# A hybrid decoder layer on one Trainium2 core: the triangular substitution of the gated DeltaNet goes from VectorE to GpSimd, with the v transposes behind the scores and four smaller edits

## The chip, the cores and the metric

One core of one Trainium2 chip runs the whole layer in one launch. The metric is the time of one execution on the device in microseconds; 0.2% of it (5 us) is about the least change that can be told from none.

The core's engines have their own in-order queues: TensorE (PE: matmuls and transposes), VectorE (DVE), ScalarE (ACT), GpSimd (POOL) and SyncE (SP, which here issues the DMAs). An instruction starts when it is at the head of its queue and what it needs is there.

## The reference, cut to what matters

2048 prompt tokens and 64 sample tokens (8 sequences of 8) go through one layer of width 1024, all in fp32:

```python
mod = silu(c) @ w_ada + b_ada                      # sh1, sc1, g1, sh2, sc2, g2
h = rmsnorm(x) * (1 + sc1) + sh1
qkv, z, b_raw, a_raw, sq, sk, sv = split(h @ w_in)
# (A) gated DeltaNet, 4 heads of 128, per chunk of C tokens:
A = where(strict, beta * (k @ k.T) * decay, 0)
T = inverse(I + A)                                 # unit lower triangular
u = T @ (v * beta) - (T @ (k * beta * exp(G))) @ S
o = (q * exp(G)) @ S + ((q @ k.T) * decay) @ u
S = S * c_dec + k_tail.T @ u
# (B) sliding-window attention, 8 q heads, 2 kv heads, window 128, sinks, relative bias
x = x + g1 * (concat(rmsnorm(o) * silu(z), attention) @ w_out)
h = rmsnorm(x) * (1 + sc2) + sh2
gate, up = split(conv3(h @ w_up) + b)              # 2 x 2816 columns
x = x + g2 * ((silu(gate) * up) @ w_down)
y = rmsnorm(x)
```

The convolutions' and the DeltaNet's states and the attention's caches are outputs as well. The part that this change moves belongs to `T = inverse(I + A)`.

## The kernel before

The tokens are worked on in two halves, in blocks of (512, 512) and of (384, 384, 320) columns. A matrix product in fp32 is done as three: each operand is split into a rounded part (`w_hi`, `hi`, by ScalarE) and the rest (`w_lo`, `lo`, by VectorE or GpSimd, line 362 for the weights), and hi·hi, lo·hi and hi·lo are summed in PSUM (line 370). In the profile `in_ps` is the in-projection, `op_ps` the out-projection, `up_ps` the up-projection of the ConvFFN. Its last columns go by a scheme of quarters (`uq_...`), for which GpSimd early and VectorE later form sums of the down-projection's weights (`weight_sums`: a unit loads `suv`, does four additions and stores `ws_d`; 11 units over `KH`).

The stages, in us of the profiled execution: start, adaLN vectors and first blocks of the in-projection 0 to 110; in-projection of half 1, with `weight_sums` on GpSimd, to 240; the first chunk's `front` and `levels` ("ahead") to 300; the mixers of half 1 beside the in-projection of half 2, to 745; out-projection of half 1 to 890; ahead and mixers of half 2 beside up-projections, then the sample tokens, to 1390; up to 1530; out-projection of half 2 to 1640; more up, then the quarters to 2110; down-projection to the end.

In the mixers, chunk c of 128 tokens runs `scan(c)` (the DeltaNet's recurrence), `attend(c)`, `levels(c+1)` and `front(c+2)` in lockstep: they are generators, one step of each in turn, and `beside` draws projection steps (the "filler") between them by a share. What is written so is input to a scheduler with a timeline of its own that then fixes the order in each engine's queue by the durations it assumes. An instruction can so land ahead of or behind others than the code says.

`front(c)` is where the change is. In order: loads `kq` (k and q, line 691) and `xv` (693); `gm` on GpSimd (697); transposes of k and q (705) and their norms (`ss`, `nr` by a power on GpSimd, 714); decays `d_ps` (724) and `Dc` (728); transposes of v (`v_ps`) and `vb`; the scores `am_ps` (744), scaled by VectorE to `AM`; `AM` to DRAM (`at_d`, 755) and back (`G`, 760) so that the eight 16 × 16 diagonal blocks of each of 4 heads stand on 32 partitions. There the unit triangular blocks are inverted by substitution: `TU` is set to the identity (memsets, GpSimd, 765, 766), its first column filled (767), then for each of 14 columns a product `gt` (772) and a subtraction into `TU` (774), each of which needs the one before, and a transposed copy (777). `TU` goes to DRAM (`tu_d`, 784, 8 DMAs) and comes back in two gathers, `T` and `inv` (799, 8 DMAs). `levels` builds the whole inverse out of these blocks in three doublings: `z_ps` and `u_ps` (line 819), where the first z needs `T<-tu_d`.

The chunk's `TU`, `G` and `xv` have one buffer each, `AM` and `vb` two, `kq` three. The product's GpSimd work in the mixers is `gm`, `nr`, `Dc`, `o` (946), `dv` (999), `PT` (1040, an operand of the attention's `pv_ps`), the convolution's small copies (586, 589) and one in ten weight splits.

Of the kernel before, what the change touches and what calls it, by code (L numbers as in the profile page):

```python
# [30 lines left out]
H = 4  # L31
# [63 lines left out]
def kernel(  # L95
# [57 lines left out]
    def ada_init(pool, tmp):  # L153
        craw = tmp.tile([P, KT, 9], F32, tag="craw", name="craw")
        nc.scalar.dma_start(craw, I["cT"])
        cT = pool.tile([P, KT, 32], F32, tag="cT", name="cT")
        bT = pool.tile([P, 48], F32, tag="bT", name="bT")
        nc.vector.memset(cT, 0.0)
        nc.scalar.activation(cT[:, :, 0:9], craw, AF.Silu)
        nc.scalar.dma_start(bT, I["b_adaT"])  # L160
        return cT, bT
# [194 lines left out]
    def load_split(src, eng=None, out=None):  # L356
        return split(load_raw(src), eng, out)
# [96 lines left out]
    def gates(hf, h, wb, pool):  # L454
# [8 lines left out]
        for bi, c0, n, np_ in blocks(hf):  # L463
# [5 lines left out]
            ev = gw.tile([P, 512], F32, tag="cv", name="ba_ev", bufs=CV)  # L469
            nc.scalar.copy(ev[:32, :n], pb[:32, :n])  # L470
            yield True
# [14 lines left out]
        nc.sync.dma_start(dt, I["dn_dt_bias"][0].partition_broadcast(P))  # L486
        nc.scalar.activation(al, al, AF.Exp)
        t0, t1, t2 = [pool.tile([P, NCH // 2 + 1, H], F32, tag=t, name=t)[:, :n_] for t in ("t0", "t1", "t2")]
# [194 lines left out]
    def front(c, d, pool, rows=P):  # L683
# [48 lines left out]
        yield True  # L732
        v_ps = bank("v_ps", "fr")
        for h in range(H):
            nc.tensor.transpose(v_ps[:rows, P * h:P * h + P], xv[:, h, :], ident)
        vb = pool.tile([P, H, P], F32, tag="vb", name="vb", bufs=two)
        nc.vector.tensor_tensor(vb[:rows], heads(v_ps)[:rows], over_i(nr[:rows, :, 0], P), ALU.mult)
        yield True

        AM = pool.tile([P, H, 2, rows], F32, tag="AM", name="AM", bufs=1 if smp else 2)  # L740
# [18 lines left out]
        for h in range(H):  # L759
            nc.sync.dma_start(G[nb * h:nb * h + nb], bass.AP(a0.tensor, a0.offset + h * rows,  # L760
                                                             [[BS * ap_ + BS, nb], [ap_, BS], [1, BS]]))
        yield True
        TU = pool.tile([4 * P // BS, 2, BS, BS], F32, tag="TU", name="TU", bufs=1)
        T0 = TU[:np_, 0]
        nc.gpsimd.memset(T0, 0.0)
        nc.gpsimd.memset(T0.rearrange("p i j -> p (i j)")[:, ::BS + 1], 1.0)
        nc.vector.tensor_scalar_mul(T0[:, 1:, 0], G[:np_, 0, 1:], -1.0)
        for j in range(1, BS - 1):
            shape = [np_, BS - 1 - j, j + 1]
            tm = pool.tile([4 * P // BS, BS * BS // 4], F32, tag="gt", name="gt")  # L770
            tv = tm[:np_, :shape[1] * shape[2]].rearrange("p (i k) -> p i k", i=shape[1])
            nc.vector.tensor_tensor(tv, G[:np_, j, j + 1:].unsqueeze(2).broadcast_to(shape),
                                    T0[:, j, 0:j + 1].unsqueeze(1).broadcast_to(shape), ALU.mult)
            nc.vector.tensor_tensor(T0[:, j + 1:, 0:j + 1], T0[:, j + 1:, 0:j + 1], tv, ALU.subtract)
            if j % 5 == 0:
                yield True
        nc.vector.tensor_copy(TU[:np_, 1], T0.rearrange("p i j -> p j i"))
        t0 = (tu_s if smp else tu_d[par])[0:1]
# [453 lines left out]
    def out_weights(hf):  # L1232

        seq = [m for o in OUT_ORDER[:len(HALVES[hf])] for m in o]
        w = {m: load_split(I["w_outT"][m]) for m in seq[:2]}
        for i, m in enumerate(seq):
            yield w[m]
            if m not in seq[i + 1:i + 3]:
                del w[m]
                new = next((x for x in seq[i + 1:] if x not in w), None)  # L1240
                if new is not None:
                    w[new] = load_split(I["w_outT"][new])
            yield
# [183 lines left out]

    RING, RING_T = 6, 1

# [3 lines left out]
    def copy_consts(dst, src):  # L1433
        for t in ("cw", "cb"):
            nc.gpsimd.tensor_copy(dst[t], src[t])
        nc.gpsimd.tensor_copy(dst["out"][:, 2 * PLAIN:], src["out"][:, 2 * PLAIN:])

# [490 lines left out]
    SHARE = (5.4, 5.5, 4.0, 2.05, (2.0, 1.4), 5.0, (1.3, 2.0), 8.0)  # L1928
    PLAIN = 3

    gate = cp.tile([P, NCH + 1, H], F32, tag="gate", name="gate")
# [9 lines left out]
    with ExitStack() as main:  # L1941
# [12 lines left out]
        with ExitStack() as es:  # L1954
# [71 lines left out]
            for bi in range(2):  # L2026
                for m in range(2):
# [5 lines left out]
            chain(*[spaced(ada_cols([(c, k + q) for q in range(4)], ac, st, at_bank), 2) for c in range(2, 6) for k in (0, 4)],  # L2033
                  spaced(weight_sums(range(6), sa, nc.gpsimd), 2)),
            chain(bias_tables(sa), gates(0, h, ic["wb"], ip), *[x_rstd(1, bi, rBs[bi], sa, st_bank) for bi in range(3)]))
# [69 lines left out]
        with ExitStack() as es:  # L2105
            sp = new_pool(es, "sp", side="right")
            beside(lockstep(sample_delta(sp), sample_attend(sp), weight_sums(range(6, KH), sp, nc.vector)), filler, SHARE[2])
        with ExitStack() as es:
            up_tags[:] = FREE_TAGS
            filler, h = between(1, filler, es, range(2 * PLAIN))  # L2110
        with ExitStack() as es:
# [5 lines left out]
            with ExitStack() as es2:  # L2117
                ts = new_pool(es2, "ts", side="right")
                beside(chain(token_sums(q, ts), W.first(PLAIN)), filler, SHARE[7])
                rest(filler)  # L2120
            uc2 = {t: tq.tile(list(a.shape), F32, tag=f"u{t}", name=f"u{t}") for t, a in uc[0].items()}
            copy_consts(uc2, uc[0])
# [107 lines left out]
```

## Time and profile before

| | |
|---|---|
| median of 3 runs | 2585.77 us (2584.51 to 2588.64) |
| profiled execution | 2588.13 us, span 2586.4 us |
| granted TensorE clock | 0.994 |
| instructions in the span | 45302 |
| TensorE busy | 2515.8 us, 97% |
| VectorE busy | 1811.4 us, 70% |
| ScalarE busy | 1286.7 us, 50% |
| GpSimd busy | 763.9 us, 30% |
| DMA | 427.62 MB, 165 GB/s over the span |

A time of the table is that of a whole execution; the span is from the first to the last instruction, 1.7 us less. Busy time counts the time in which an engine has an instruction of its own under way, not whether the end waits for it. In the rows of the profile, PE is TensorE, PEld its weight loads, DVE VectorE, ACT ScalarE, POOL GpSimd, and SPq a DMA issue of SyncE; a group's row ends, behind the mean duration in ns, with the idle time ahead of it and what ended that.

### The profile page before, as it was taken

What the parts mean: (1) busy time and instruction counts of PE and PEld (TensorE: products, weight loads), DVE (VectorE), ACT (ScalarE), POOL (GpSimd) and SP (SyncE); (2) the same over time, 40 slices, a digit from 0 to 9 for tenths busy, and PEclk for the clock granted to TensorE, in tenths of its full rate; (3) what the DMA queues carried; (4) which work ended last, traced back from release to release, by engine and by line L of the source; (5) the groups of instructions that cost most, each with busy time, mean ns of one, the idle gap of its engine ahead of it and who ended that gap; (6) DMA issues with size and microseconds to landing.
All of it is one profiled execution on the core that took longest, in us unless ns stands there. A gap on an engine that the chain in (4) does not pass through costs nothing.

```text
span 2586.4 us, 45302 instructions
## 1 busy us (share of the span) xinstructions
PE 2515.8 (97%) x16410; PEld 2211.3 (85%) x16410; DVE 1811.4 (70%) x3621; ACT 1286.7 (50%) x3133; POOL 763.9 (30%) x697
## 2 busy tenths in 40 slices
PE   7999999999999999999999999999999999999998
PEld 5777888888988787787887789999999998888998
DVE  6465579897543677788758665886776666687676
ACT  5554365554343455465544353655555554454453
POOL 2064143323232422222111123345555520021012
PEclk9999999999999999999999999999999999999999
DMA  7887553343555353443346267325555448676463
GB/s 278 281 297 255 159 141 112 101 120 93 128 178 203 109 150 96 107 104 100 88 163 200 80 219 225 112 78 164 174 174 183 160 168 293 213 242 201 138 193 133
DMA packets 315852, 427.62 MB, mean 165 GB/s; under 512 B 82243, under 2 KB 206244, under 8 KB 315364
## 3 DMA queue, kind: packets, MB, share of 16 engines
q1 hardware_dynamic: 315052, 423.55, 51.8%
q8 instruction: 129, 2.11, 0.3%
q0 software_dynamic: 288, 1.11, 0.1%
q14 instruction: 95, 0.78, 0.1%
q10 hardware_dynamic: 288, 0.06, 0.0%
HBM read 305.07 MB, written 120.57 MB: 165 GB/s over the span
## 4 chain that ended last, share of the span: by engine, by line
PE 75%; DVE 11%; DMA 6%; ACT 3%; issue 2%; POOL 2%; SPq 1%; DVEq 0%; POOLq 0%; ACTq 0%
PE up_ps L370 19%; PE dn_ps L1850 17%; PE in_ps L370 8%; PE op_ps L370 6%; PE uq_b L1632 6%; PE uq_c L1632 3%; DVE ev L581 3%; PE uq_u L1632 2%; PE uq_g L1632 2%; PE uq_a L1632 1%; PE as_ps L1009 1%; DMA wada<-in_w_ada_dram 1%; PE pv_ps L1047 1%; PE u_ps L819 1%; DVE w_lo L362 1%
## 5 line engine op out<-in xcount | busy, mean ns | idle before, releaser
L370 PE MATMUL in_ps<-hi,w_hi 128*128 128x512 f32 (+2 forms) x880 | 319.4, 366 | 2.5 <-ACT hi L301 1.9
L370 PE MATMUL in_ps<-lo,w_hi 128*128 128x512 f32 (+2 forms) x880 | 315.6, 359 | 3.1 <-DVE lo L302 2.0
L370 PE MATMUL up_ps<-hi,w_hi 128*128 128x512 f32 (+2 forms) x808 | 313.0, 388 | 1.5 <-ACT sg L576 1.5
L370 PE MATMUL in_ps<-hi,w_lo 128*128 128x512 f32 (+2 forms) x880 | 314.0, 357 | 0.5 <-POOL w_lo L362 0.5
L370 PE MATMUL up_ps<-lo,w_hi 128*128 128x512 f32 (+2 forms) x808 | 312.1, 387 | 1.9 <-DVE lo L302 1.9
L370 PE MATMUL up_ps<-hi,w_lo 128*128 128x512 f32 (+2 forms) x808 | 311.0, 386 | 0.1
L1850 PE MATMUL dn_ps<-tl,wh 128*128 128x512 f32 (+2 forms) x796 | 271.6, 341 | 0.0
L1850 PE MATMUL dn_ps<-th,wh 128*128 128x512 f32 (+2 forms) x796 | 269.9, 341 | 0.0
L1850 PE MATMUL dn_ps<-th,wl 128*128 128x512 f32 (+2 forms) x796 | 268.7, 341 | 0.0
L361 ACT CAST w_hi<-w_raw 128x1024 fp32r<-128x1024 f32 x126 | 132.1, 1049 | 145.9 <-PE op_ps L370 63.0
L362 DVE TENSOR_TENSOR w_lo<-w_raw,w_hi 128x1024 fp32r<-128x1024 f32 x115 | 145.3, 1264 | 84.1 <-ACT w_hi L361 78.3
L370 PEld LDWEIGHTS in_ps<-lo,w_hi 128*128 128x128 f32 x880 | 166.9, 190 | 23.1 <-issue 3.4
L370 PEld LDWEIGHTS in_ps<-hi,w_hi 128*128 128x128 f32 x880 | 166.2, 190 | 23.2 <-issue 3.6
L370 PEld LDWEIGHTS up_ps<-hi,w_hi 128*128 128x128 f32 x808 | 152.3, 188 | 35.2 <-issue 7.3
L370 PEld LDWEIGHTS up_ps<-lo,w_hi 128*128 128x128 f32 x808 | 152.4, 189 | 33.4 <-issue 6.4
L370 PEld LDWEIGHTS in_ps<-hi,w_lo 128*128 128x128 f32 x880 | 166.5, 189 | 15.9 <-issue 1.0
L370 PEld LDWEIGHTS up_ps<-hi,w_lo 128*128 128x128 f32 x808 | 152.1, 188 | 27.9 <-issue 1.6
L1734 ACT CAST wh<-wr 128x512 fp32r<-128x512 f32 x149 | 92.2, 619 | 154.8 <-PE dn_ps L1850 101.6
L581 DVE SCALAR_TENSOR_TENSOR ev<-rb,cw,ev 128x512 f32<-128x512 f32 (+2 forms) x180 | 142.6, 797 | 35.2 <-ACT ev L574 31.5
L1850 PEld LDWEIGHTS dn_ps<-tl,wh 128*128 128x128 f32 x796 | 150.5, 189 | 15.7 <-DVE tl L1735 0.3
L1850 PEld LDWEIGHTS dn_ps<-th,wl 128*128 128x128 f32 x796 | 150.4, 189 | 15.2
L1850 PEld LDWEIGHTS dn_ps<-th,wh 128*128 128x128 f32 x796 | 150.2, 189 | 15.5
(574 smaller groups left out, 6414.6 us busy)
## 6 DMA issues: line engine op xcount, KB each, us to landing
w_raw<-in_w_upT_dram SPq DMA_DIRECT2D x50, 512.0 KB
wada<-in_w_ada_dram SPq DMA_DIRECT2D x48, 512.0 KB
w_raw<-in_w_inT_dram SPq DMA_DIRECT2D x44, 512.0 KB
wr<-ws_d SPq DMA_DIRECT2D x88, 256.0 KB
w_raw<-in_w_outT_dram SPq DMA_DIRECT2D x34, 512.0 KB
d<-act_d SPq DMA_DIRECT2D x33, 512.0 KB
wr<-in_w_downT_dram SPq DMA_DIRECT2D x66, 256.0 KB
proj<-ev SPq DMA_DIRECT2D x44, 256.0 KB
```

What stands on the lines that cost most here:

```text
L361: nc.scalar.copy(hi, raw)
L362: (eng or nc.vector).tensor_tensor(lo, raw, hi.bitcast(F32), ALU.subtract)
L370: nc.tensor.matmul(ps[:, :n], a[:, k, :], b[:, k, :n], start=first is not False and k == ks[0] and i == 0, stop=last is not False and k == ...
L581: nc.vector.scalar_tensor_tensor(out, src(j), w[:, j:j + 1], out, ALU.mult, ALU.add)
L819: mm = lambda out, a, b, r, c: nc.tensor.matmul(out, a, b, start=True, stop=True, tile_position=(r, c))
L1009: nc.tensor.matmul(banks[v][:, 256 * g:256 * g + 256 - P * k0], qs[:, 2 * (g0 + g) + v], t[:, v, :2 - k0].rearrange("p w j -> p (w j)"), s ...
L1047: mm = nc.tensor.matmul(pv_ps[64 * v:64 * v + 64, :], (vprev[0], vt if k0 else dv)[half][:, 64 * v:64 * v + 64], PT[v, half], start=half = ...
L1632: nc.tensor.matmul(bk[t][:, :nb], u[:, k], v[:, k], start=new and k == 0 and y == 0, stop=k == KG - 1 and y == 2, skip_group_check=True)
L1734: nc.scalar.copy(h, raw)
L1850: nc.tensor.matmul(acc[m, s][:, :n], w[q, i][a][:, c], th[b][:, v], start=new and i == 0 and y == 0, stop=i == KH - 1 and y == 2, skip_gro ...
```

## The change

1. `front`: the v transposes and `vb` stand behind the scores, the store of `at_d` and the loads of `G`.
2. `front`: the substitution's 1 first column, 28 products and subtractions and 1 transposed copy go from VectorE to GpSimd (17 calls: 16 chunks and the sample).
3. At the start ScalarE takes a Silu of a constant before `craw` has come in; in `gates` the Exp of `al` is held behind the copy `held`. Both change which tables ScalarE loads: in its program the loads go from 13 to 10.
4. `out_weights`: in the second half every other of the later `w_out` splits has its `w_lo` on GpSimd (8 of them).
5. `RING_T` 1 → 2: two weight tiles of the quarters are prepared ahead instead of one. `uc2["out"]` shrinks to the part that is copied.
6. `FEW = 5`: five units of weight sums on GpSimd at the start (six before), the other six on VectorE beside the sample's steps.

```diff
+        warm = tmp.tile([P, 16], F32, tag="warm", name="warm")
+        nc.scalar.activation(warm, mhalf, AF.Silu)
...
-            nc.scalar.copy(ev[:32, :n], pb[:32, :n])
+            held = nc.scalar.copy(ev[:32, :n], pb[:32, :n]).ins
...
-        nc.scalar.activation(al, al, AF.Exp)
+        with tc.issue_after(held):
+            nc.scalar.activation(al, al, AF.Exp)
...
-        v_ps = bank("v_ps", "fr")
-        for h in range(H):
-            nc.tensor.transpose(v_ps[:rows, P * h:P * h + P], xv[:, h, :], ident)
-        vb = pool.tile([P, H, P], F32, tag="vb", name="vb", bufs=two)
-        nc.vector.tensor_tensor(vb[:rows], heads(v_ps)[:rows], over_i(nr[:rows, :, 0], P), ALU.mult)
-        yield True
...
             nc.sync.dma_start(G[nb * h:nb * h + nb], bass.AP(a0.tensor, a0.offset + h * rows,
                                                              [[BS * ap_ + BS, nb], [ap_, BS], [1, BS]]))
         yield True
+        v_ps = bank("v_ps", "fr")
+        for h in range(H):
+            nc.tensor.transpose(v_ps[:rows, P * h:P * h + P], xv[:, h, :], ident)
+        vb = pool.tile([P, H, P], F32, tag="vb", name="vb", bufs=two)
+        nc.vector.tensor_tensor(vb[:rows], heads(v_ps)[:rows], over_i(nr[:rows, :, 0], P), ALU.mult)
+        yield True
...
-        nc.vector.tensor_scalar_mul(T0[:, 1:, 0], G[:np_, 0, 1:], -1.0)
+        nc.gpsimd.tensor_scalar(T0[:, 1:, 0], G[:np_, 0, 1:], -1.0, 1.0, ALU.mult, ALU.mult)
...
-            nc.vector.tensor_tensor(tv, G[:np_, j, j + 1:].unsqueeze(2).broadcast_to(shape),
+            nc.gpsimd.tensor_tensor(tv, G[:np_, j, j + 1:].unsqueeze(2).broadcast_to(shape),
                                     T0[:, j, 0:j + 1].unsqueeze(1).broadcast_to(shape), ALU.mult)
-            nc.vector.tensor_tensor(T0[:, j + 1:, 0:j + 1], T0[:, j + 1:, 0:j + 1], tv, ALU.subtract)
+            nc.gpsimd.tensor_tensor(T0[:, j + 1:, 0:j + 1], T0[:, j + 1:, 0:j + 1], tv, ALU.subtract)
...
-        nc.vector.tensor_copy(TU[:np_, 1], T0.rearrange("p i j -> p j i"))
+        nc.gpsimd.tensor_copy(TU[:np_, 1], T0.rearrange("p i j -> p j i"))
...
-                    w[new] = load_split(I["w_outT"][new])
+                    w[new] = load_split(I["w_outT"][new], nc.gpsimd if hf and i % 2 else None)
...
-    RING, RING_T = 6, 1
+    RING, RING_T = 6, 2
...
-        nc.gpsimd.tensor_copy(dst["out"][:, 2 * PLAIN:], src["out"][:, 2 * PLAIN:])
+        late = lambda a: a[:, a.shape[1] - MU + 2 * PLAIN:]
+        nc.gpsimd.tensor_copy(late(dst["out"]), late(src["out"]))
...
+    FEW = 5
...
-                  spaced(weight_sums(range(6), sa, nc.gpsimd), 2)),
+                  spaced(weight_sums(range(FEW), sa, nc.gpsimd), 2)),
...
-            beside(lockstep(sample_delta(sp), sample_attend(sp), weight_sums(range(6, KH), sp, nc.vector)), filler, SHARE[2])
+            beside(lockstep(sample_delta(sp), sample_attend(sp), weight_sums(range(FEW, KH), sp, nc.vector)), filler, SHARE[2])
```

All lines behind the first edit move by 2 to 5 numbers: the substitution's lines 765 to 777 are 767 to 779 in the changed kernel, `kq`'s load 694, `nr` 717, `Dc` 731, `PT` 1042, `dv` 1001.

How the queues change, at two places. The first is VectorE's queue in the second half's mixers, before, from the first column of chunk 14's substitution on (`ss`, `bn`, `r` belong to the norms of this and another chunk):

```order
L767 TENSOR_SCALAR TU<-G 32x15
L143 TENSOR_SCALAR rsq<-ss_13230 128x4
L772 TENSOR_TENSOR gt<-G,TU 32x28
L774 TENSOR_TENSOR TU<-TU,gt 32x14x2
L712 TENSOR_SCALAR ss<-ss 128x8
L772 TENSOR_TENSOR gt<-G,TU 32x39
L716 RECIPROCAL bn<-ss 128x4
L774 TENSOR_TENSOR TU<-TU,gt 32x13x3
L717 TENSOR_TENSOR bn<-bn,beta 128x4
L772 TENSOR_TENSOR gt<-G,TU 32x48
L945 TENSOR_TENSOR r_13239<-r_13239,nr 128x4
L718 TENSOR_TENSOR bn<-bn,tail 128x4
```

Other VectorE work stands between the steps of the chain. GpSimd's queue in the changed kernel, at the end of the same chunk's substitution:

```order
L776 TENSOR_TENSOR TU<-TU,gt 32x4x12
L1042 TENSOR_TENSOR PT<-pt,cst 128x512
L774 TENSOR_TENSOR gt<-G,TU 32x39
L717 TENSOR_TENSOR nr<-ss,halves 128x8
L776 TENSOR_TENSOR TU<-TU,gt 32x3x13
L731 TENSOR_TENSOR Dc<-Dc,cst 128x512
L774 TENSOR_TENSOR gt<-G,TU 32x28
L1042 TENSOR_TENSOR PT<-pt,cst 128x512
L776 TENSOR_TENSOR TU<-TU,gt 32x2x14
L774 TENSOR_TENSOR gt<-G,TU 32x15
L776 TENSOR_TENSOR TU<-TU,gt 32x15
L779 COPY TU<-TU 32x256
```

The chain now shares its queue with `PT`, `nr` and `Dc`, which stood there before without it.

The second place is SP's queue ahead of the load of the first chunk's k and q, before (`suv` and `ws_d` are the load and the store of a weight-sums unit, `proj<-ev` a store of the in-projection):

```order
L1676 DMA suv<-in_w_downT_dram 128x1024 x2
L353 DMA w_raw<-in_w_inT_dram 128x1024
L643 DMA proj<-ev 128x512 x2
L1685 DMA ws_d<-suv 128x1024 x2
L353 DMA w_raw<-in_w_inT_dram 128x1024
L691 DMA kq<-proj 128x4x128 x2
L693 DMA xv<-proj 128x4x128
```

and in the changed kernel:

```order
L646 DMA proj<-ev 128x512
L1688 DMA ws_d<-suv 128x1024 x2
L646 DMA proj<-ev 128x512
L355 DMA w_raw<-in_w_inT_dram 128x1024
L646 DMA proj<-ev 128x512
L694 DMA kq<-proj 128x4x128 x2
L696 DMA xv<-proj 128x4x128
```

The sixth unit's load and store are gone from here; three other DMAs now stand between the fifth unit's store and `kq`, where one stood behind the sixth's.

More of the change, by code (lines that the diff above doesn't have):

```diff
@@ L2120 @@
                 rest(filler)
-            uc2 = {t: tq.tile(list(a.shape), F32, tag=f"u{t}", name=f"u{t}") for t, a in uc[0].items()}
+            shape = lambda t, a: [P, MU - 2 * PLAIN, 18] if t == "out" else list(a.shape)
+            uc2 = {t: tq.tile(shape(t, a), F32, tag=f"u{t}", name=f"u{t}") for t, a in uc[0].items()}
             copy_consts(uc2, uc[0])
```

## The prediction

> **What bounds the kernel now.** I read the busy shares first, then the table by stage, then what TensorE (PE) waits for in each stage, and last one chunk's chain in order of time.
>
> ```profile
> PE 2515.8 (97%) x16410; PEld 2211.3 (85%) x16410; DVE 1811.4 (70%) x3621; ACT 1286.7 (50%) x3133; POOL 763.9 (30%) x697
> 300.00:745.00 445.00, 426.21 (x3545) 385.90 (x3544) 326.31 (x946) 227.48 (x736) 131.04 (x132) 0.99 0.43 120
> 890.00:1300.00 410.00, 406.86 (x3060) 327.21 (x3060) 329.80 (x905) 221.85 (x700) 91.12 (x89) 0.99 0.41 107
> ```
>
> The first row is the whole span, the other two (length, then busy PE, PEld, DVE, ACT, POOL, granted clock, DMA share, GB/s) are the mixers of the first and of the second half. TensorE is busy 97% of the span. VectorE (DVE) has 326.3 of 445.0 us in the first mixers and 329.8 of 410.0 in the second, GpSimd (POOL) 131.0 and 91.1. Taking work off VectorE can pay only where TensorE waits for VectorE; those waits, the first mixers' and then the second's (total us, times, longest):
>
> ```profile
> PE u_ps L819 <- DVE Y L869: 4.1, 2, 3.0
> PE z_ps L819 <- DVE T L842: 3.5, 2, 2.3
> PE pv_ps L1047 <- POOL PT L1040: 2.2, 2, 1.4
> PE z_ps L819 <- DVE T L861: 2.1, 3, 1.4
> PE o_ps L921 <- DVE S L915: 1.8, 2, 1.1
> PE pt_ps L1036 <- DVE nl L1029: 1.6, 2, 1.1
> PE o_ps L901 <- DVE vb L896: 1.1, 1, 1.1
> PE ot_ps L951 <- POOL o L946: 0.6, 1, 0.6
> ...
> PE z_ps L819 <- DMA T<-tu_d: 0.5, 1, 0.5
> ```
> ```profile
> PE o_ps L901 <- DVE vb L896: 0.5, 1, 0.5
> ```
>
> Six VectorE rows of the first mixers sum to 14.2 us (4.1 + 3.5 + 2.1 + 1.8 + 1.6 + 1.1); in the second mixers it is 0.5. So the most that a freer VectorE can give there is 14.7 us, 0.6% of the time, and the substitution's own chain hardly shows: `T<-tu_d`, its last transfer, costs 0.5 us in all.
>
> **The substitution, moved.** Removed from VectorE:
>
> ```profile
> L774 DVE TENSOR_TENSOR TU<-TU,gt 32x28 f32<-32x28 f32 (+5 forms) x238 | 58.5, 246 | 4.8
> L772 DVE TENSOR_TENSOR gt<-G,TU 32x28 f32<-32x28 f32 (+5 forms) x238 | 55.8, 234 | 4.9
> L767 DVE TENSOR_SCALAR TU<-G 32x15 f32<-32x15 f32 (+1 forms) x17 | 7.1, 417 | 18.1 <-DMA G<-at_d 18.0
> L777 DVE COPY TU<-TU 32x256 f32<-32x256 f32 (+1 forms) x17 | 6.3, 371 | 0.4
> ```
>
> 58.5 + 55.8 + 7.1 + 6.3 = 127.7 us in 17 calls, 7.5 us each. About 60 us leave each half's VectorE, which falls from some 73% to 60% of the first mixers. I let that end half of the 14.2 us of waits: the 3.0 and 2.3 us ones stand behind several VectorE operations in a row, while the rest are single operations that TensorE needs at once. Gain 7 us (0 to 14), and 0.5 in the second mixers.
>
> GpSimd never ran these shapes in the profile. Its nearest rows, and two lone steps of the weight sums:
>
> ```profile
> L1040 POOL TENSOR_TENSOR PT<-pt,cst 128x512 f32<-128x512 f32 x32 | 45.3, 1418 | 113.8 <-ACT pt L1039 113.8
> L999 POOL TENSOR_TENSOR dv<-vt 128x128 f32<-128x128 f32 x15 | 9.3, 618 | 71.7 <-ACT vt L992 71.7
> 183.39 1.26 POOL L1679 TENSOR_TENSOR suv<-suv 128x512 f32<-128x512 f32 x1
> 184.72 1.34 POOL L1680 TENSOR_TENSOR suv<-suv 128x512 f32<-128x512 f32 x1
> ```
>
> From 618 ns at 128 elements a partition to 1418 at 512 the slope is 2.08 ns per element and the intercept 352 ns. The 14 steps' shapes run 28, 39, 48 ... 64 ... 28, 15; they sum to 665 elements, 47.5 each, so 352 + 99 = 451 ns, and 70 ns to the next dependent operation (183.39 + 1.26 to 184.72). 28 × 0.52 = 14.6, and about 0.9 for the first operation and the transposed copy: 15.5 us a chunk. Bounds: all 30 at VectorE's own 246 ns, 30 × 0.32 = 9.5; all at 618, 30 × 0.69 = 20.6. These means already hold whatever GpSimd loses to VectorE today. Into the chain the new order puts other GpSimd work, four in the piece shown above (two PT, nr and Dc, the last two taken at PT's 1.4 us); over the chunks of the mixers I count two of them in the mean, 3 us. So the chain takes 18.5 us from G to TU (12.5 to 24).
>
> The Trainium skill, "GPSIMD Engine Reference", section 4.1, says to keep elementwise work on VectorE, since a two-input operation is about twice as slow on GpSimd; the busy times agree with that here (451 against the 240 ns of L772 and L774), but the chain's length also counts what stands between the operations.
>
> Does a chain of 18.5 us come too late? Chunk 14 before:
>
> ```profile
> 1192.03 1.03 PE L744 MATMUL am_ps<-kq 128*128 128x256 f32 x4
> 1195.15 0.56 SPq L755 DMA_DIRECT2D at_d<-AM  x1
> 1202.32 0.17 DVE L767 TENSOR_SCALAR TU<-G 32x15 f32<-32x15 f32 x1 [0.73 <-DMA G<-at_d]
> 1222.85 0.37 DVE L777 COPY TU<-TU 32x256 f32<-32x256 f32 x1
> 1222.87 3.10 SPq L784 DMA_DIRECT2D tu_d<-TU  x8
> 1227.50 1.73 SPq L799 DMA_DIRECT2D T<-tu_d  x4
> 1230.69 0.44 PE L819 MATMUL z_ps<-T,AM 32*32 32x16 f32 x32
> 1198.48 4.13 PE up_ps L370 x18
> ```
>
> On VectorE the chain took 20.9 us (1202.32 to 1223.22) for 7.5 us of work: it stood between other VectorE work. Over the mixers' chunks it is about 17. After it come 7.5 us of transfers, and z starts at most 1.5 us behind the last T issue (1229.23 to 1230.69): TensorE's order puts z right at the landing, so what the chain gains in length becomes a wait. GpSimd's chain is 18.5 − 17 = 1.5 us longer. On the credit side, scores ahead of the v transposes let at_d leave earlier; of the 2.1 us between the scores' end (1193.06) and at_d I credit 0.5. On the debit side the new order of TensorE has fewer projection matmuls between a chunk's last scores and its z: counted in it, 116 → 105 in the mean of chunks 8 to 15 and 127 → 124 in chunks 2 to 7. One is 229 ns (4.13 / 18), so z comes 2.4 and 0.6 us sooner. With a margin of 1.5 us the first half is 1.5 − 0.5 + 0.6 − 1.5 = 0.1 us late, the second 1.9. At the lower bound for GpSimd (6 us shorter) none is late. I take half: 1 us for 8 chunks, 8 in all; bounds 0 and 30. PT and o, which TensorE already waits for (2.2 + 0.6), now stand behind substitution steps: 2 us more (0 to 6), unless GpSimd stalls on their inputs, which is in the slower rival.
>
> **v behind the scores.** The four transposes stay, no TensorE work goes; its effect is the 0.5 above. If vb comes later, the scan's vb row (1.1 us) is what would grow. 0.
>
> **FEW = 5.** The sixth unit of weight sums leaves GpSimd and SP ahead of the first chunk's load:
>
> ```profile
> 234.62 1.69 SPq L1685 DMA_DIRECT2D ws_d<-suv  x2
> ...
> 236.86 1.47 SPq L691 DMA_DIRECT2D kq<-proj  x2
> 242.70 1.93 PE L705 MATMUL kq_ps<-cst,kq 128*128 128x128 f32 x8 [4.49 <-DMA kq<-proj]
> ```
>
> TensorE waits 4.49 us for kq, whose issue stands behind ws_d on SP. Without ws_d kq can leave 1.7 us sooner, and the stores that were behind the GpSimd unit some more; but TensorE's order asks for kq sooner as well. Gain 3 (0.5 to 4.5). The unit then runs on VectorE in the sample stage, beside a TensorE that never waits for it there: 0; without that cover about 8 us.
>
> **warm and held.** They take 3 of 13 table loads off ScalarE. One is
>
> ```profile
> 27.90 1.28 ACT L487 ACT_TABLE_LOAD   x1
> PE ss_ps L219 <- DVE xst L339: 10.0, 1, 10.0
> ```
>
> 3 × 1.28 = 3.8 us of ScalarE, but at the start TensorE's long wait (second row) is for VectorE; 0.5 (0 to 2.6, two loads).
>
> **w_lo on GpSimd, second out-projection; RING_T = 2.** Here GpSimd takes 8 splits:
>
> ```profile
> L362 POOL TENSOR_TENSOR w_lo<-w_raw,w_hi 128x1024 fp32r<-128x1024 f32 x11 | 27.2, 2471 | 36.3 <-ACT w_hi L361 36.3
> PE op_ps L370 <- DVE w_lo L362: 2.0, 2, 1.3
> PE uq_b L1632 <- DVE rl L1488: 1.5, 1, 1.5
> ```
>
> A block of that stage is 24 matmuls of 384 columns, 24 × 229 × 384 / 512 ns = 4.1 us by the duration above, and two blocks pass between splits on GpSimd, so 2.47 us fits; VectorE's 2.0 us wait may go or turn into one for GpSimd: 0 (−2 to +5). The ring of two has the quarters' second tile ready while VectorE is free: the 1.5 us wait goes (0 to 1.5).
>
> **Sum** against the profiled execution, 2588.1 us: −0.5 − 3 − 7 − 0.5 − 1.5 + 8 + 2 = −2.5, so 2585.6. That execution is 2.4 above the median of the runs, so a median of 2583, 0.1% below. What a measurement can tell here is about 0.2%, 5 us.
>
> **Rivals.** *The chain is in time* (GpSimd near its lower bound): the +8 goes and PT's and o's 2 stay. −12.5 + 2 = −10.5 with half of VectorE's waits gone, 2575; −17.7 with all of them gone, 2568. For it: GpSimd's 30% busy share, and a chain that no longer stands between other VectorE work; against: PT and o already keep TensorE waiting 2.8 us with 131 us of work on GpSimd.
>
> *The chain is late in most chunks* (slower). The place is z behind `T<-tu_d`, once per chunk, 14 times in the mixers. Each us of lateness in the mean costs 14; above a mean of 1.1 us (−10.5 + 14 × 1.1 = +5) the kernel is slower by more than can be measured, and by the working above that is a mean chain from 18.6 us on. For it: that is my own full sum before I took half of it (0.1 and 1.9 us late), and GpSimd's queue is in order, so a substitution step behind PT stands still until PT's input is there (113.8 us of such idle time before 32 PT, 3.6 each, in the row above). Against: the order places what it places by due times, and before the transfer was late by 0.5 us only. At 1.6 us, −10.5 + 22.4 = +12, 2598; at 2 us +17.5, 2603.
>
> A sharper form, with its row, VectorE's weight splits:
>
> ```profile
> L362 DVE TENSOR_TENSOR w_lo<-w_raw,w_hi 128x1024 fp32r<-128x1024 f32 x115 | 145.3, 1264 | 84.1 <-ACT w_hi L361 78.3 <-DMA toep<-toep_ev 4.4
> ```
>
> If three of a chunk's 30 steps meet such a split on VectorE and wait for half of it, 0.6 us each, the chain is 1.9 us longer and z 3 us late in the mean: −10.5 + 42 = +31.5, 2617. The GpSimd means that I took hold some of that already, so I give it 0.04 of the slower case's chance. The Trainium skill, "SBUF — State Buffer", section "Who interferes with whom", has a rule for it: a VectorE operation with two SBUF inputs and a GpSimd operation that reads SBUF exclude each other for the whole instruction. By that rule it would be the common case; no row of before shows it apart from other delays.
>
> *Nothing measurable moves, for another reason*: VectorE's waits were never due to its load and stay, and z is 0.4 us late: −5.5 + 5.5, the median as before.
>
> **Chances.** Forecast with the last rival, 0.36; chain in time 0.33; late 0.31, the sharp form in it. By the bounds, 2580.6 and 2590.9: faster 0.34, same 0.35, slower 0.31. The range goes from the first rival's 2568 to the late case's 2603; the forecast's own is 2578 to 2590.
>
> **What would show it.** After: VectorE some 60 us less busy in either mixers, GpSimd some 120 us more over both; G-to-TU walls of 15 to 22 us; DVE rows of the first mixers' waits halved; rows "z_ps <- T<-tu_d" of 5 to 12 us in total. Right for the rest: the kq wait under 2 us, uq_b's gone. I am wrong if T<-tu_d stays under 2 us and the DVE waits vanish (faster), or if it exceeds 20 us (slower), or if GpSimd waits pv_ps, ot_ps and op_ps together exceed 10.

## The result, and the profile after

The changed kernel is slower: 2606.64 us median (2600.05 to 2610.97, 4 runs) against 2587.2 us, ratio 1.0067 [1.0049, 1.0086], which is +17 us (the two medians are 19.4 apart). The forecast of 2583 is wrong, in its sign and in its range (2568 to 2603). The profiled execution has a span of 2604.4 us, 18.0 us more than before, and a granted clock of 0.991 in place of 0.994.

The busy row and the two mixers in the same windows as before (length, busy PE, PEld, DVE, ACT, POOL, granted clock, DMA share, GB/s):

```profile
PE 2524.1 (97%) x16410; PEld 2218.3 (85%) x16410; DVE 1728.2 (66%) x3106; ACT 1286.7 (49%) x3131; POOL 974.3 (37%) x1212
300.00:745.00 445.00, 432.43 (x3512) 393.92 (x3511) 297.81 (x734) 233.50 (x743) 203.82 (x329) 0.99 0.44 122
890.00:1300.00 410.00, 393.98 (x2965) 315.10 (x2965) 277.84 (x636) 214.52 (x672) 182.39 (x320) 0.98 0.39 104
```

VectorE is relieved by 28 and 52 us in the two windows and GpSimd takes 73 and 91 more. Over the whole span VectorE's busy time fell by 83.2 us, not by the 127.7 of the rows removed: before, 27 of these overlapped other VectorE records, and VectorE's other work is 17 us longer now. TensorE's waits, the first mixers' and then the second's:

```profile
PE z_ps L821 <- DMA T<-tu_d: 6.7, 4, 3.3
PE z_ps L821 <- DVE T L844: 1.5, 1, 1.5
...
PE u_ps L821 <- ACT Y L853: 0.9, 1, 0.9
```
```profile
PE z_ps L821 <- DMA T<-tu_d: 7.4, 3, 2.7
PE pv_ps L1049 <- POOL PT L1042: 3.5, 1, 3.5
PE u_ps L821 <- DVE Y L871: 2.3, 2, 2.1
PE o_ps L903 <- DVE vb L898: 1.5, 2, 1.2
```

The VectorE waits of the first mixers are nearly gone (2.7 us, 14.2 before), and `T<-tu_d` has taken their place: 6.7 us there and 7.4 in the second mixers, 14.1 against 0.5. Stages compare best from landmark to landmark of TensorE's own work, since a fixed window holds different work in two kernels. The time at which the trace has TensorE at each, and the difference to before (the fourth is the start of the second out-projection's last matmul):

| TensorE reaches | before | after | e1 | e2 | e5 | e9 |
|---|---|---|---|---|---|---|
| first out-projection | 770.6 | −8.2 | −10.1 | +7.1 | −10.5 | −7.4 |
| first chunk of the second half | 911.2 | −9.8 | −11.7 | +5.5 | −12.7 | −7.4 |
| second out-projection | 1530.7 | +11.7 | −7.9 | +20.0 | −8.2 | −1.3 |
| last matmul of it | 1632.1 | +21.1 | +3.4 | +20.6 | −6.9 | +13.8 |
| first matmul of the down phase | 2123.9 | +18.6 | +1.1 | +20.3 | −6.5 | +14.3 |

Each column is one execution. TensorE's order up to the first out-projection is the same in the changed kernel and in e3, e4, e6, e9 and e12, and their executions reach that point 3.9 to 13.1 us ahead of before: a difference of a few us between columns there tells nothing. A stage's own length is steadier: e1, e3 and e5 have one order from the first chunk of the second half to the second out-projection, and take 623.3, 624.2 and 623.9 us for it.

Up to the second half the changed kernel is 9.8 us ahead. It loses 21.5 us in the second half's ahead, mixers and sample, and 9.4 in the second out-projection, and gets 2.5 back up to the down phase. The two stages that lose, before and then after:

```profile
911.20:1530.70 619.50, 615.93 (x4093) 487.08 (x4092) 470.46 (x1156) 312.86 (x927) 122.47 (x107) 1.00 0.43 125
1530.70:1632.10 101.40, 99.41 (x600) 98.44 (x599) 65.58 (x101) 47.84 (x79) 40.25 (x33) 1.00 0.71 225
```
```profile
901.30:1542.30 641.00, 622.98 (x4092) 491.53 (x4091) 431.16 (x890) 315.27 (x926) 236.95 (x377) 0.99 0.42 124
1542.30:1653.30 111.00, 102.81 (x601) 99.87 (x600) 65.66 (x94) 48.03 (x80) 60.03 (x43) 0.98 0.65 206
```

Only part of the 21.5 us is idle time: TensorE stood idle 3.6 us in this stage before (619.5 − 615.9) and 18.0 after, 14.4 more, and it was busy 7 us longer for the same matmuls. That second part is a lower clock, as one late z shows (chunk 11; start, duration, work, and in brackets the wait; then the window from 1099 to 1102 us, with the clock in its third column from the end):

```profile
1094.94 0.39 PE L372 MATMUL up_ps<-lo,w_hi 128*128 128x512 f32 x1
1097.80 0.44 PE L821 MATMUL z_ps<-T,AM 32*32 32x16 f32 x32 [2.47 <-DMA T<-tu_d]
...
1101.11 0.63 PE L372 MATMUL up_ps<-hi,w_lo 128*128 128x512 f32 x1
1101.54 0.63 PE L372 MATMUL up_ps<-hi,w_hi 128*128 128x512 f32 x1
...
1102.37 0.39 PE L372 MATMUL up_ps<-hi,w_lo 128*128 128x512 f32 x1
1102.60 0.40 PE L372 MATMUL up_ps<-hi,w_hi 128*128 128x512 f32 x1
```
```profile
1099.00:1102.00 3.00, 3.00 (x14) 2.81 (x14) 0.67 (x2) 1.56 (x4) 0.00 (x0) 0.50 0.71 197
```

After the wait of 2.47 us the granted clock is 0.50 for some 3.4 us, and the projection's matmuls start every 0.43 us in place of 0.23. The wait so costs 1.7 us more. There are five such stretches in the second mixers of the changed kernel (at 973, 1048, 1099, 1150 and 1232 us) and one before. Three stand behind waits for `T<-tu_d` (2.25, 2.47 and 2.72 us), the first behind a wait of 3.54 for PT and the last behind one of 2.15 for `Y`.

### The profile page after: what moved, and what is told of

It is laid out like the page before. It is cut to its first block, busy times and chain, and to the rows that moved or that the text cites. A ratio compares the mean times of both kernels' runs of the same rounds, so it can differ in the third digit from the quotient of the medians.

```text
span 2604.4 us, 45274 instructions
## 1 busy us (share of the span) xinstructions
PE 2524.1 (97%) x16410; PEld 2218.3 (85%) x16410; DVE 1728.2 (66%) x3106; ACT 1286.7 (49%) x3131; POOL 974.3 (37%) x1212
## 4 chain that ended last, share of the span: by engine, by line
PE 69%; DVE 9%; DMA 7%; POOL 6%; issue 3%; ACT 2%; SPq 2%; POOLq 0%; DVEq 0%; ACTq 0%
PE dn_ps L1853 17%; PE up_ps L372 14%; PE in_ps L372 10%; PE uq_b L1635 6%; PE op_ps L372 4%; PE uq_c L1635 3%; PE uq_u L1635 2%; PE uq_g L1635 2%; POOL TU L776 2%; POOL gt L774 2%; DVE ev L584 2%; PE uq_a L1635 1%; DMA wada<-in_w_ada_dram 1%; DVE w_lo L364 1%; PE as_ps L1011 1%
## 5 line engine op out<-in xcount | busy, mean ns | idle before, releaser
L364 DVE TENSOR_TENSOR w_lo<-w_raw,w_hi 128x1024 fp32r<-128x1024 f32 x106 | 137.5, 1297 | 96.6 <-ACT w_hi L363 90.4
L1737 ACT CAST wh<-wr 128x512 fp32r<-128x512 f32 x149 | 92.1, 619 | 154.1 <-PE dn_ps L1853 102.8
L1853 PEld LDWEIGHTS dn_ps<-tl,wh 128*128 128x128 f32 x796 | 150.5, 189 | 15.4
```

The costliest lines, as they stand in the source:

```text
L364: (eng or nc.vector).tensor_tensor(lo, raw, hi.bitcast(F32), ALU.subtract)
L1737: nc.scalar.copy(h, raw)
L1853: nc.tensor.matmul(acc[m, s][:, :n], w[q, i][a][:, c], th[b][:, v], start=new and i == 0 and y == 0, stop=i == KH - 1 and y == 2, skip_gro ...
```

## The experiments

All ratios are to the kernel before, timed in turn on the same chip; the change, e1 to e4, e5 to e8, e9 to e11 and e12 were timed in five sessions, so ratios compare between them and medians don't.

| run | what it is | median us | ratio [95%] |
|---|---|---|---|
| after | the change | 2606.64 | 1.0067 [1.0049, 1.0086] |
| e1 | after, substitution on VectorE | 2585.44 | 0.9985 [0.9973, 0.9997] |
| e2 | before, substitution on GpSimd | 2607.42 | 1.0069 [1.0056, 1.0083] |
| e3 | after, substitution on GpSimd in the first half only | 2588.05 | 1.0001 [0.9986, 1.0015] |
| e4 | after, w_lo of w_out on VectorE | 2599.2 | 1.0041 [1.0026, 1.0057] |
| e5 | e1 and e4 together | 2578.25 | 0.9964 [0.9951, 0.9977] |
| e6 | after, more projection work in the second mixers | 2616.1 | 1.0105 [1.0090, 1.0119] |
| e7 | after, nr scaled on GpSimd | 2616.89 | 1.0109 [1.0094, 1.0124] |
| e8 | before, v behind the scores | 2584.3 | 0.9981 [0.9971, 0.9991] |
| e9 | after, levels written later in the second half | 2603.95 | 1.0056 [1.0037, 1.0074] |
| e10 | before, tables, RING_T, FEW | 2575.92 | 0.9952 [0.9936, 0.9968] |
| e11 | before, FEW alone | 2580.54 | 0.9969 [0.9956, 0.9982] |
| e12 | e9 and e4 together | 2596.74 | 1.0029 [1.0014, 1.0045] |

**e1: the substitution back on VectorE.**

```diff
-nc.gpsimd.tensor_scalar(T0[:, 1:, 0], ...)   # and the 28 tensor_tensor and the tensor_copy
+nc.vector.tensor_scalar_mul(T0[:, 1:, 0], ...)
```

> The changed kernel with the substitution back on VectorE, all other edits kept. Theory A (the loss is made by the substitution on GpSimd in the second half's mixers, 21.5 us from the second ahead to the second out-projection, and by w_lo on GpSimd in that out-projection, 9.4 us; the first half's mixers gain 5.6 us by it): the second half's loss goes and so does the first half's gain; 2587 - 2.7 (front, kq) + 9.4 - 2.6 (quarters and after) = 2591 us, with z_ps <- T<-tu_d back under 2 us and VectorE's wait for nr (20.8 us in the second mixers) back near 0. Rival B (the v transposes behind the scores or the smaller edits make the loss): about 2605 us, with the waits for T<-tu_d kept.

2585.44 us, ratio 0.9985: 21 us of the ratio go with this one part (1.0067 − 0.9985 = 0.0082). The wait for `T<-tu_d` is 0.9 us in the second mixers and does not reach the listed rows of the first. Not as expected: the early lead stays. e1 is 10.1 us ahead at the first out-projection, so the 8.2 us of the changed kernel there need no relief of VectorE. The waits for VectorE in the first mixers are down to some 4 us with the substitution on VectorE:

```profile
PE in_ps L372 <- ACT ev L577: 3.1, 3, 1.9
PE o_ps L903 <- DVE vb L898: 1.5, 1, 1.5
PE u_ps L821 <- DVE Y L871: 1.0, 1, 1.0
PE in_ps L372 <- ACT sb L590: 0.9, 1, 0.9
```

**e2: the substitution on GpSimd, alone.** The kernel before with the reverse of e1's edit.

> The kernel before with the substitution on GpSimd and nothing else. Theory A: -6 us in the first mixers, +21 in the second, so 2587 + 15 = 2602 us, with VectorE waiting some 20 us for nr in the second mixers and z_ps <- T<-tu_d at 10 us or more. Rival B (the other edits make the loss): 2580 to 2588 us.

2607.42 us, 1.0069: the whole loss, with nothing else changed. It loses in both mixers, 9 us in the first as well, where a gain of 6 was expected. In the second, 14.5 us are lost up to the second out-projection with only 4.3 of waits for `T<-tu_d`, where 10 or more were expected, and VectorE's waits for `nr` are 8.9, not 20. The first mixers' window and its two largest waits:

```profile
300.00:745.00 445.00, 426.30 (x3494) 386.65 (x3493) 287.92 (x733) 225.57 (x731) 201.64 (x341) 0.97 0.43 117
```
```profile
PE z_ps L819 <- DMA T<-tu_d: 12.6, 5, 4.1
PE as_ps L1009 <- DVE nl L1019: 2.1, 1, 2.1
```

VectorE has 38 us less to do than before in this window, and TensorE is no better off: 12.6 us of waits for `T<-tu_d` stand where 14.2 for VectorE stood, and the clock is 0.97 in place of 0.99.

**e3: on GpSimd in the first half only.**

```diff
+on_pool = c < NCH // 2
+eng = nc.gpsimd if on_pool else nc.vector   # for all of the chunk's substitution
```

> The changed kernel with the substitution on GpSimd in the first half's eight chunks alone, on VectorE in the second half's and the sample's. Theory A: the first half keeps its 9.8 us, the second mixers lose nothing, the second out-projection its 9.4: 2587 - 9.8 + 9.4 - 2.6 = 2584 us. Rival B: 2605 us. Rival C (GpSimd's work of the substitution is paid wherever it runs, by collisions with VectorE): no gain is left in the first half against e1, so 2591 us.

2588.05 us, 1.0001, against 0.9985 of e1: no gain from GpSimd in the first half, as rival C had it (the intervals overlap). Whether by the collisions that it named is not shown: TensorE's waits for `T<-tu_d` in the first mixers are 7.5 us here and 0.5 in e1.

**e4: w_lo of w_out on VectorE.**

```diff
-w[new] = load_split(I["w_outT"][new], nc.gpsimd if hf and i % 2 else None)
+w[new] = load_split(I["w_outT"][new])
```

> The changed kernel with every w_lo split of w_out on VectorE again, the substitution on GpSimd. Theory A: the 9.4 us that the second out-projection lost come back, 2597 us, with the waits op_ps <- w_lo at 2 to 3 us in all. Rival (that stage is only late because its weights or the mixers' last results come in another order, w_lo on GpSimd is hidden): 2606 us.

2599.2 us, 1.0041: 0.0026 or 6.7 us come back (the two intervals overlap), and the second out-projection is as long as before:

```profile
1545.20:1646.90 101.70, 99.28 (x601) 98.52 (x600) 64.19 (x101) 47.95 (x79) 40.95 (x33) 1.00 0.72 224
```

What the splits on GpSimd made late, by the waits of the changed kernel from 1542 to 1654 us, and last ScalarE's wait for the raw weights in this kernel and in e4:

```profile
PE rb_ps L229 <- DVE dg L225: 2.8, 3, 2.1
PE op_ps L372 <- DVE w_lo L364: 2.8, 2, 2.6
PE op_ps L372 <- POOL w_lo L364: 2.1, 2, 1.6
```
```profile
ACT w_hi L363 <- DMA w_raw<-in_w_outT_dram: 20.7, 7, 6.7
```
```profile
ACT w_hi L363 <- DMA w_raw<-in_w_outT_dram: 8.6, 4, 3.0
```

TensorE waits 7.7 us for three different things, all short. That the next raw weights come later because GpSimd holds their buffer 2.45 us instead of 1.26 fits the last two rows, but wasn't tried by itself.

**e5: both back on VectorE.** e1's and e4's edits.

> The changed kernel with the substitution and all w_lo splits of w_out back on VectorE; left of the change are v behind the scores, the two table edits, RING_T and FEW. Theory A (two edits lose, each by itself: the substitution on GpSimd some 20 us, w_lo on GpSimd 9 to 11 us in the second out-projection; the others gain): e1 stood 7.9 us ahead of the kernel before at the second out-projection, and the quarters gain 2 more: 10 us faster, ratio 0.996. Rival (the gain of e1 up to that point is given back later, by a stage that then waits for something else): ratio 0.9985 as e1.

2578.25 us, 0.9964, as expected: each of the two parts loses by itself, and what is left of the change gains 9 us. The second out-projection takes 102.8 us. In the seven profiles with these splits on VectorE and nothing moved later (before, e2, e4, e5, e8, e10, e11) it takes 101.4 to 103.3, with them on GpSimd (after, e1, e3) 111.0 to 112.7.

**e6: more projection work in the second mixers.**

```diff
-beside(mixers(1, mp), filler, SHARE[2])
+beside(mixers(1, mp), filler, 5.2)
```

> The changed kernel with more projection work drawn between the steps of the second half's mixers (5.2 for 4.0), so that 111 matmuls in place of 105.5 stand between a chunk's last scores and its z in the mean of chunks 8 to 15. Theory A (z is placed too early for GpSimd's chain, and each wait of over 2 us is followed by 3.4 us at half clock): 5.6 x 0.23 = 1.3 us a chunk later, so T<-tu_d's 7.4 us in the second mixers and the half-clock stretches behind it mostly go: 8 us less than the changed kernel, ratio 1.004. Rival B (VectorE's operations, stretched and held up by GpSimd, set the end, wherever z stands): ratio 1.0065 to 1.007.

2616.1 us, 1.0105, slower than either theory had it. `T<-tu_d` falls to 2.3 us in the second mixers as expected and the half-clock stretches there from five to two. But the projection work drawn earlier is missing at the end of the stage, where it covered the way to the second out-projection:

```profile
1542.59 1.01 PE L372 MATMUL op_ps<-mixh,w_hi 128*128 128x384 f32 x2 [11.66 <-ACT mixh L1226]
```

An idle time of 11.66 us, with 17.1 us at half clock around it: the gain was given back at once. The run says nothing against theory A, but doesn't show it.

**e7: nr scaled on GpSimd.** The other thing that I saw in the changed kernel was VectorE's queue standing still for `nr`, whose power waits in GpSimd's queue among the substitution steps:

```profile
DVE nr L733 <- POOL nr L717: 20.8, 7, 5.0
```

```diff
-nc.vector.tensor_scalar_mul(nr[:rows, :, 0], ...); nc.vector.tensor_scalar_mul(nr[:rows, :, 1], ...)
+nc.gpsimd.tensor_scalar(nr[:rows, :, 0], ...); nc.gpsimd.tensor_scalar(nr[:rows, :, 1], ...)
```

> The changed kernel with the two small multiplications of nr on GpSimd, behind its power, in place of VectorE. Theory D (VectorE's queue stands still for nr, 20.8 us in 7 waits of the second mixers, and what is behind it comes late: AM, the levels' operations): those waits vanish, and 6 to 8 us of the second mixers' loss with them, ratio 1.004; the order of TensorE moves too, z 6.5 matmuls later, so a gain alone doesn't tell D from A, but no gain would speak against both. Rival E (GpSimd's queue is longer by 16 operations, and all behind them later): ratio 1.007 or above.

2616.89 us, 1.0109. VectorE's wait for `nr` is gone, and nothing is gained by that; theory D falls, and rival E's ratio came. By the words of the expectation, a run without a gain also speaks against theory A, since z comes 6.4 matmuls or 1.5 us later here (chunks 8 to 15). The trace has why it needn't: GpSimd's chain is 1.7 us longer and the copy, counted from the scores, 2.1 us later, so the later place is used up. TensorE's waits of the second mixers are longer:

```profile
PE z_ps L821 <- DMA T<-tu_d: 9.9, 5, 3.1
PE pv_ps L1049 <- POOL PT L1042: 5.9, 2, 4.0
```

**e8: v behind the scores, alone.** The kernel before with the block of `v_ps` and `vb` moved, as in the change.

> The kernel before with the v transposes and vb behind the scores, nothing else. If the 10 us that e1 gained up to the first out-projection come from this edit, some 7 of them show here (the rest is the kq wait, which stays): 2587 - 7, ratio 0.997, VectorE-named waits of the first mixers at 5 us or less in place of 14. If they come from the smaller edits: ratio 1.000.

2584.3 us, 0.9981 [0.9971, 0.9991]: 5 us by itself. In its profile, which is of the slowest of its twelve executions (2592.24 us), the first mixers wait 4.9 us for VectorE by name, so that row came as expected, though its time is between the two theories.

**e9: levels written later.** Four empty steps ahead of `levels` in the second half's mixers; the work and its share are as in the changed kernel.

```diff
-g.append(levels(ds[c + 1], pool))
+g.append(chain((True,) * (4 if hf else 0), levels(ds[c + 1], pool)))
```

> The changed kernel with four empty steps ahead of each levels() of the second half's mixers, so that z is written later: in chunks 10 to 15 the order has 113 matmuls of the projection between a chunk's last scores and its z, 99.5 in the changed kernel, and the share of projection work drawn is as it was. Theory A (z too early for GpSimd's chain: waits for T<-tu_d, and 3.4 us at half clock behind each wait of over 2 us): z comes 13.8 x 0.23 = 3.2 us later, the 7.4 us of waits and four or five half-clock stretches of 1.7 us each in the second mixers go, up to 14 us: ratio 1.0015 to 1.003. Rival B (GpSimd's work delays VectorE's and the levels' own chain as a whole, so what z doesn't wait for is waited for later): ratio 1.006 or above.

2603.95 us, 1.0056, less than expected, and as near to rival B's 1.006; but the stage did what theory A said:

```profile
PE z_ps L821 <- DMA T<-tu_d: 2.4, 3, 1.2
PE z_ps L821 <- DVE T L844: 1.8, 1, 1.8
```
```profile
903.80:1529.40 625.60, 615.34 (x4093) 486.72 (x4092) 439.48 (x886) 311.12 (x921) 235.99 (x376) 1.00 0.43 124
1529.40:1645.90 116.50, 105.22 (x600) 102.78 (x599) 68.13 (x99) 50.39 (x85) 62.02 (x45) 0.96 0.67 212
```

The stage takes 625.6 us in place of 641.0, its clock is 1.00 again, and no half-clock stretch lies in these mixers. Of the 21.5 us that the changed kernel lost there, 15.4 came back with the levels later: 7.8 of idle time and 7.6 of slow clock. Not all of it is z, since the waits for PT and `Y`, with their stretches, are nearly gone too. The second out-projection then takes 116.5 us, 5.5 more than in the changed kernel, with three half-clock stretches in place of one. So part of what z doesn't wait for is waited for later, as rival B had it: against the changed kernel the run gains 0.0011 or 3 us, and the intervals overlap.

**e12: e9 with w_lo on VectorE.**

> e9 with w_lo of w_out on VectorE: the substitution on GpSimd in all chunks, z written later, no split of w_out on GpSimd in the second half. Theory A (the substitution on GpSimd loses only by z's place, and w_lo on GpSimd only in the second out-projection, where e9 lost 15 us): e9 stood 1.3 us ahead of the kernel before at that stage, and it now passes it at no loss: level with the kernel before, ratio 0.998 to 1.000, the second out-projection 101 to 104 us long instead of 116.5. Rival (e9's loss there came from the levels being late, not from GpSimd's splits): 110 us or more in that stage, ratio 1.004 or above.

2596.74 us, 1.0029 [1.0014, 1.0045]. Its two stages, and last the first of them in e4, which differs from e12 by the place of the levels alone:

```profile
906.90:1537.80 630.90, 618.79 (x4092) 488.10 (x4091) 440.88 (x885) 311.32 (x922) 239.35 (x376) 0.99 0.42 124
1537.80:1644.30 106.50, 101.64 (x601) 99.93 (x601) 69.31 (x107) 50.28 (x84) 42.13 (x35) 0.98 0.73 227
```
```profile
902.40:1545.20 642.80, 622.90 (x4092) 491.32 (x4091) 430.93 (x890) 315.31 (x927) 234.69 (x377) 0.99 0.42 124
```

The mixers' stage again takes less with the levels later, 11.9 us, in the same TensorE order as e9's. The out-projection is down to 106.5 us, nearer to theory A than to the rival, but the ratio is neither's. In the time of the whole run the levels' place gives 0.0012 against e4, 3 us as in e9, and again the intervals overlap. So it is shown in the stage and not in the whole. With z later and without the splits, GpSimd's substitution still costs some 17 us against e5 (0.0065). In the traces 7.0 of them lie in the mixers' stage, 3.7 in the second out-projection and 8.4 ahead of the second half, where nothing was moved in e12 and executions of one order differ by as much; their cause is open.

**e10 and e11: the smaller edits.** e10 is the kernel before with `warm`, `held`, `RING_T` and `FEW`; e11 has `FEW = 5` alone.

> The kernel before with the two table edits, RING_T 2 and FEW 5, without v behind the scores, without w_lo on GpSimd, the substitution on VectorE. If the edits add up (e5 0.9964, v alone 0.9981), these make 0.9983, some 4.5 us: the kq wait of 4.5 us gone and 1 to 2 us at the quarters. Rival (they pay only together with v behind the scores): ratio 0.9995 to 1.000.

> The kernel before with FEW 5 alone. As in the prediction: -3 us (0.5 to 4.5), by the kq wait of 4.5 us, which falls under 1.5; a half-clock stretch of 3.4 us behind that wait goes as well, 1.7 more: ratio 0.998. Rival (TensorE's order asks for kq earlier, and the wait stays): 1.000.

e11: 2580.54 us, 0.9969, 8 us. The load of kq leaves 11.8 us earlier, and TensorE no longer waits:

```profile
229.06 1.03 PE L705 MATMUL kq_ps<-cst,kq 128*128 128x128 f32 x8
225.04 0.92 SPq L691 DMA_DIRECT2D kq<-proj  x2
```

Before, these rows stood at 242.70 with a wait of 4.49, and at 236.86. Besides the wait, the half-clock stretch right behind it (at 242.8 us before) is gone, and the waits that the first mixers had for VectorE are shorter too (6.3 us in place of 14.2), though this edit leaves the mixers' code alone. e10: 2575.92 us, 0.9952, nearly three times the gain expected, the fastest version here and faster than both kernels; its interval overlaps e11's and e5's. So v behind the scores adds nothing that shows to the smaller edits (e5 against e10).

## Why the prediction was wrong

The parts as measured: smaller edits −12 us (e10, 0.0048), v on top of them 0 to +3 (e5 against e10), w_lo on GpSimd +5 to +7 (e5 against e1, after against e4), substitution on GpSimd +21 (after against e1). From before over e10, e5 and e1 to after these are the steps of one row of kernels, so that they add up to the +17 is no test. The substitution has one: alone on the kernel before it costs +18 (e2), on e5 +20 (e4 against e5). The prediction's terms for it were +8, +2, −7 and −0.5, in sum +2.5.

- **z late, +8, "I take half".** This is the step that failed most. The full working gave lateness 0.1 and 1.9 us for the halves; halving it had no row behind it. And the price of lateness was wrong: I counted the wait alone. The trace shows `T<-tu_d` at 14.1 us, and behind each of its four waits of over 2 us a stretch of half clock that costs 1.7 or 3.4 us more. In the second half's stage, moving the levels took 12 and 15 us off; the rest of the +18 to +21 is not explained by any run here. My rival of a late chain had the mechanism and the place, and should have been the forecast. That its time was near (2598 to 2603) is in part luck: it took 1.6 to 2 us of lateness a chunk, while the measured 14.1 us over 14 chunks are 1.0, which by its own price gives 2589, and things that it had at nothing (the half clock, w_lo) or that are open made up the rest. My signs missed it for the same reason: `T<-tu_d` stayed under the 20 us that were to mean slower, and the named waits for GpSimd are 5.8, not over 10.
- **Why it is late.** Not by a longer chain. From first column to copy it took 17.2 us in the mean of chunks 2 to 15, and 17.8 on VectorE before; I had 18.5 and 17. In the second half it is the order: 105 projection matmuls stand between a chunk's last scores and its z in the mean of chunks 8 to 15, 115 before. I had that term (2.4 us). In e9 it is 115 again, and the waits go although the chain there is 21.2 us. Besides, `at_d` leaves 4.9 us behind the scores in these chunks, 3.2 before, where I credited 0.5 us for an earlier store; how much of the waits that makes is not shown. In the first mixers, with 6.7 us of the waits, the order lost 3 matmuls only and no run moved z; there the cause is open.
- **VectorE's relief, −7.** Wrong: no gain is left to see. Half of the waits were said to end with a freer VectorE. They fall to some 4 and 6 us in e1 and e11 with VectorE as loaded as before; in e2, with VectorE relieved, they fall to 4 as well, but 12.6 us of waits for `T<-tu_d` came in their place.
- **A GpSimd step, 451 + 70 ns.** Somewhat high: the two rows below give 375 ns, 1.6 times VectorE's 240, and 78 to the next, so 12.7 us and with the copy 14 for the chain (15.5 predicted), within the bounds.

```profile
L776 POOL TENSOR_TENSOR TU<-TU,gt 32x28 f32<-32x28 f32 (+5 forms) x238 | 95.1, 400 | 16.8
L774 POOL TENSOR_TENSOR gt<-G,TU 32x28 f32<-32x28 f32 (+5 forms) x238 | 83.6, 351 | 17.2
```

- **PT and o, +2.** About right in the mixers of the changed kernel: PT 3.7 us in all, o none that is listed, against 2.8 before; the half clock behind the one long wait for PT is not in it.
- **FEW, −3.** Right in mechanism, too small: −8 (−11 to −5), since the wait takes a half-clock stretch with it and the first chunk starts earlier.
- **w_lo on GpSimd, 0.** Wrong: +5 to +7, beyond my bound of +5 or at it. I asked only whether 2.47 us fit between two blocks; the trace has TensorE waiting for either engine's splits, and ScalarE for the raw weights, 20.7 us against 8.6 in e4.
- **v behind the scores, 0.** −5 alone, none beside FEW.
- **RING_T, −1.5.** The wait is gone from the changed kernel's trace (one of 1.1 us stands in e5's), and the quarters are 2.2 us shorter in the changed kernel, but 0.6 longer in e5; not told apart.

## What to carry to other kernels

On a path where TensorE's order puts a matmul right at the landing of its operand, moving the work behind that operand to another engine can move the matmul too: look at what the new order puts between, before the new engine's speed. Price a wait of TensorE of over 2 us with the slow stretch that mostly follows it, 1.7 us here. A relief of an engine is worth only waits that an experiment ends by that relief; here they also ended by an earlier start, and new waits took their place. And see that what a stage gains reaches the end: of 12 to 15 us in the mixers' stage some 3 did, too few to be told from none.

## What the runs showed of the hardware

**The clock after a wait.** In the profiles of before, after and e9, every idle time of TensorE of 2.5 us or more behind the kernel's start was followed, within some 1.5 us, by 3.4 or 6.8 us at a granted clock of 0.50; of those from 1.5 to 2.4 some were. That is no sharp limit: over all fourteen profiles, between 60 us and the kernel's end, such a stretch began in, or within 2.4 us behind, 20 of 28 waits of 2.0 to 2.5 us, 5 of 9 of 2.5 to 2.65, and all but one of the 34 longer ones (one of 3.34 in e4 had none). The Trainium skill, "TensorE: Matmul & The Clock Gate", in "What's actually happening", gives an idle window of about 3.4 us for the clock to fall to half; here the fall came after waits of 2.2 to 2.7 us already (2.47 in the row above), so the measured waits decide. The shortest slow stretches, 3.4 us, are as long as that window.

**GpSimd and VectorE.** A substitution step that meets no VectorE operation took 264 ns in the mean (136 of 448 steps); beside operations of VectorE with one operand in PSUM the means are the same, 210 to 275; beside the convolution's `ev<-rb,cw,ev`, with all operands in SBUF, it is 496, and beside w_lo splits, which read two operands in SBUF, 862 (each step put down to the VectorE operation that overlaps it longest). One such meeting, two GpSimd rows and the VectorE row:

```profile
1138.63 0.20 POOL L774 TENSOR_TENSOR gt<-G,TU 32x15 f32<-32x15 f32 x1
1140.04 1.19 POOL L776 TENSOR_TENSOR TU<-TU,gt 32x15 f32<-32x15 f32 x1
1138.39 2.77 DVE L364 TENSOR_TENSOR w_lo<-w_raw,w_hi 128x1024 fp32r<-128x1024 f32 x1 [2.46 <-ACT w_hi L363]
```

A step of 0.2 us takes 1.19, and the split of 1.26 takes 2.77 (one other took 2.46, the rest 1.2 to 1.3). Each of the twelve splits that met a chunk's substitution in the changed kernel had a step of 1.16 to 1.32 us beside it. That is the exclusion of the Trainium skill, "SBUF — State Buffer", "Who interferes with whom", to whose full price I had given 0.04 of the slower case. The traces agree with it as a rule, and its price in the chain is small: by an estimate from the means 375 − 264 = 111 ns a step, 3 us a chunk, with 12 such splits met in 16 chunks where the rival took three in each; and the chain on GpSimd was still no longer than on VectorE.
